# A dilated convolution: one of sixteen output images is stored in three transfers instead of one

## The chip, the cores and the metric

The kernel runs on one core of one Trainium2 chip. The metric is the device time of one execution in microseconds (us), as the median of several runs. Profiles are of one execution each.

## The reference

A 3x3 convolution with dilation 2 and zero padding of 2, in float32: 16 images of 64 channels and 64 x 64 pixels become 16 images of 128 channels of the same size.

```python
batch, c_in, h, w, c_out, k, dilation = 16, 64, 64, 64, 128, 3, 2
...
x_pad = np.pad(x, ((0, 0), (0, 0), (pad, pad), (pad, pad)), mode='constant')
...
output[b, co] += weight[co, ci, kh, kw] * x_pad[b, ci, kh*dilation:kh*dilation+h, kw*dilation:kw*dilation+w]
```

The inputs are 16.8 MB and the outputs 33.6 MB, so the kernel moves some 50 MB between memory and the core.

## The kernel before

The images are taken in eight pairs (`pb` = 0 to 7). A pair of input images of 64 channels fills the 128 partitions; TensorE works on both halves in turn (`hb` = 0, 1), 64 rows of the array for each.

Loads. The weights (line 63) and the pairs 0, 1 and 2 (line 71) are loaded from SyncE's queue, pair 0 in four pieces. Pair `pb + 3` is loaded from ScalarE's queue when pair `pb` begins. There are three float32 input buffers. GpSimd (line 126) and ScalarE (line 129) turn each pair into three float16 planes: even row groups, odd row groups, and their sum.

Weights. They are transposed by TensorE (line 106) into five slots: three rows of the 3x3 filter and two differences of rows. With the sum plane, an output row group takes five products instead of six: the one with the sum is shared by two row groups.

Main loop. Each pair has four units (`u`), each of 16 output rows for both images. In each unit TensorE (line 160) makes the shared product, which ScalarE copies out of the accumulator (line 181), then the two groups of difference products, to which VectorE adds the shared part (line 187) as it writes the result into the output buffer `o` of the image, 128 partitions (one for each output channel) of 64 x 64 float32. There are six such buffers, two for each pair.

Stores. After the last unit of a pair, SyncE issues the store of both images (line 198), 2 MB each: image `2 * pb + hb`, 128 rows of 16,384 bytes, one for each partition. The last pair is stored in two halves, after its second and its fourth unit, so the whole program has 18 stores. SyncE issues them in program order. Each waits for VectorE's last write into the buffer, and for the earlier transfer that had the same completion semaphore: the transfers of the program use eight of these in turn.

The order of the instructions is that of the program as written (a manual schedule).

Of the kernel before, what the change touches and what calls it, by code (L numbers as in the profile page):

```python
# [10 lines left out]
def kernel(  # L11
# [7 lines left out]
    nc = tc.nc  # L19

    B, CI, H, W = x.shape
# [5 lines left out]
    P = 128  # L27
    f32 = mybir.dt.float32
    f16 = mybir.dt.float16
    NP = B // 2  # L30
# [11 lines left out]
    NB = UQ * QW  # L42
    UR = 2 * UQ
    KWS = (1, 0, 2)

    SLOT = {"w0": 0, "w1": 1, "w2": 2, "w21": 3, "w01": 4}
    NS = len(SLOT)
# [20 lines left out]
    def load(pb, cuts, eng):  # L68
        x32[pb] = x32pool.tile([P, H, W], f32, tag="x32", name=f"x32_{pb}")
        for lo, hi in zip(cuts, cuts[1:]):  # L70
            eng.dma_start(out=x32[pb][:, lo:hi], in_=x_pair[pb, :, lo:hi])  # L71
# [21 lines left out]
    for name, a in (("w21", 2), ("w01", 0)):  # L93
        for u in range(2):
            nc.vector.tensor_sub(  # L95
                out=w16[:, SLOT[name] * KW : (SLOT[name] + 1) * KW, u, :],
# [5 lines left out]
    for n, name in enumerate(("w1", "w21", "w0", "w01", "w2")):  # L102
        ps = cpool.tile([P, NB], f32, tag="ps", name=f"wt{n}")
        k0 = SLOT[name] * KW
        for j in range(KW):
            nc.tensor.matmul(  # L106
                out=ps[:, j * CO : (j + 1) * CO],
# [12 lines left out]
    def prepare(pb, lo, hi):  # L120
        if pb not in x16:
            x16[pb] = x16pool.tile([P, 3, 2 * NQ, W], f16, tag="x16", name=f"x16_{pb}")
        q0, q1 = lo // 4, hi // 4
        src = x32[pb].rearrange("p (q e r) w -> p q e (r w)", e=2, r=2)
        dst = x16[pb].rearrange("p e (q r) w -> p q e (r w)", r=2)
        nc.gpsimd.tensor_add(  # L126
            out=dst[:, q0:q1, 2, :], in0=src[:, q0:q1, 0, :], in1=src[:, q0:q1, 1, :]
        )
        nc.scalar.copy(out=dst[:, q0:q1, 0:2, :], in_=src[:, q0:q1, :, :])  # L129
# [4 lines left out]
    def conv(pb, hb, ps, u, terms):  # L134
# [4 lines left out]
        for name, e, shift in terms:  # L139
            for kw in KWS:  # L140
                dw = (kw - 1) * d
# [14 lines left out]
    def phase(pb, u, terms):  # L156
        ps = [cpool.tile([CO, NB], f32, tag="ps", name=f"ps{hb}") for hb in range(2)]
        for pair in zip(*(conv(pb, hb, ps[hb], u, terms) for hb in range(2))):
            for m in pair:
                nc.tensor.matmul(**m)  # L160
        return ps

    for pb in range(NP):
        o = [
            opool.tile([P, H, W], f32, tag="o", name=f"o{pb}_{hb}") for hb in range(2)
        ]
        ov = [t.rearrange("p (q e r) w -> p q e (r w)", e=2, r=2) for t in o]
        last = pb == NP - 1
        for u in range(NU):
            if u == 0 and pb + 3 < NP:  # L170
                load(pb + 3, [0, H], nc.scalar)
            if pb + 1 < NP:
                if u == 1:
                    prepare(pb + 1, 0, 36)
                elif u == 2:
                    prepare(pb + 1, 36, H)

            s32 = []
            for hb, ps in enumerate(phase(pb, u, [("w1", 2, 0)])):
                s = spool.tile([P, NB], f32, tag="s32", name=f"s32_{hb}")  # L180
                nc.scalar.copy(out=s, in_=ps)  # L181
                s32.append(s)
            for e, terms in enumerate(
                ([("w21", 1, 0), ("w0", 1, -1)], [("w01", 0, 0), ("w2", 0, 1)])
            ):
                for hb, ps in enumerate(phase(pb, u, terms)):
                    nc.vector.tensor_add(  # L187
                        out=ov[hb][:, u * UQ : (u + 1) * UQ, e, :],
                        in0=ps.rearrange("p (q c) -> p q c", c=QW),
                        in1=s32[hb].rearrange("p (q c) -> p q c", c=QW),  # L190
                    )


            step = NU // 2 if last else NU
            if (u + 1) % step == 0:
                fl = slice((u + 1 - step) * 4 * UQ, (u + 1) * 4 * UQ)
                for hb in range(2):
                    nc.sync.dma_start(out=out[2 * pb + hb, :, fl], in_=o[hb][:, fl])


# [33 lines left out]
```

## Time and profile before

| | |
|---|---|
| time, median of 3 runs | 129.29 us (128.47 to 130.64) |
| the profiled execution's own time | 130.13 us |
| its span, first to last instruction | 128.3 us |
| moved by DMA | 50.77 MB, mean 396 GB/s |
| stores of 2,048 KB (14), issue to landing | 20.4 us, median |
| stores of 1,024 KB (4), issue to landing | 15.5 us, median |
| TensorE busy | 105.4 us (82%) |
| VectorE busy | 83.1 us (65%) |
| ScalarE busy | 67.4 us (52%) |
| GpSimd busy | 38.5 us (30%) |

The span is what the profile shows of an execution; the time has some 1.8 us more around it. An engine's busy time is a mean over the span. The page also cuts the span in 40 slices with a digit for each engine (tenths of the slice that it was busy), and gives the same for the core's 16 DMA engines, which carry out all transfers whatever engine issues them. A store's time to landing runs from its issue to the last of its sixteen completion marks, so it holds the time that it stands in the queue behind earlier transfers.

### The profile page before, as it was taken

The page shows a single profiled execution, that of the slowest core. Times are in us where ns is not written, and L with a number is a line of the kernel's source. Part 1 is how long each engine was busy: PE and PEld are TensorE (multiplying, and loading weights), DVE is VectorE, ACT ScalarE, POOL GpSimd, SP SyncE. Part 2 cuts the span into 40 slices and gives each one's busy share as a digit, 9 for nine tenths or more (in the row PEclk, how much of TensorE's full clock was granted, in tenths as well). Part 3 has the DMA queues.
Part 4 walks back from the last instruction along what each step waited for, and adds up shares of the span by engine and source line. Part 5 has one row for each costly group of instructions (what it writes and reads, how often), then busy time and mean ns, then how long its engine had stood idle before and what let it go on. Part 6 is the DMA issues. An engine that isn't in the chain of part 4 may idle for free.

```text
span 128.3 us, 2442 instructions
## 1 busy us (share of the span) xinstructions
PE 105.4 (82%) x981; PEld 55.3 (43%) x981; DVE 83.1 (65%) x136; ACT 67.4 (52%) x87; POOL 38.5 (30%) x24
## 2 busy tenths in 40 slices
PE   6399979999999999999999999999999999300000
PEld 2164425655565555555555555555556555100000
DVE  0550759887788778777877749978777777700000
ACT  3778597496359537933883398339833333000000
POOL 2095391499467006700860094000000000000000
PEclk9999999999999999999999999999999999995555
DMA  4999999998999999999999999999999999999940
GB/s 126 300 462 419 424 444 424 383 296 373 424 444 424 416 426 434 419 439 439 409 434 429 444 409 434 439 419 414 439 449 409 424 444 424 414 424 421 429 186 13
DMA packets 4330, 50.77 MB, mean 396 GB/s; under 512 B 480, under 2 KB 480, under 8 KB 1120
## 3 DMA queue, kind: packets, MB, share of 16 engines
q1 hardware_dynamic: 3600, 40.14, 74.6%
q10 hardware_dynamic: 720, 10.49, 20.4%
q8 instruction: 7, 0.11, 0.3%
q14 instruction: 3, 0.02, 0.0%
HBM read 17.07 MB, written 33.55 MB: 394 GB/s over the span
## 4 chain that ended last, share of the span: by engine, by line
PE 75%; ACT 7%; DMA 2%; DVE 1%; issue 1%; DVEq 0%; ACTq 0%
PE ps L160 74%; ACT x L129 3%; DMA w<-in_weight_dram 2%; ACT w L92 2%; ACT s L181 2%; PE wt L106 1%; DVE o L187 1%; DVEq L229 0%; ACT w_sb L117 0%; ACTq L71 0%; ACTq L181 0%; DVEq L187 0%
## 5 line engine op out<-in xcount | busy, mean ns | idle before, releaser
L160 PE MATMUL ps<-x,w_sb 64*128 64x496 f16 (+2 forms) x960 | 100.9, 368 | 1.6 <-ACT s L181 1.2
L187 DVE TENSOR_TENSOR o<-ps,s 128x512 f32<-128x512 f32 x128 | 79.5, 683 | 23.7 <-PE ps L160 14.8
L160 PEld LDWEIGHTS <-w_sb 64*128 64x128 f16 x960 | 53.0, 94 | 49.3 <-issue 3.9
L181 ACT COPY s<-ps 128x512 f32<-128x512 f32 x64 | 34.4, 589 | 36.6 <-issue 20.3
L126 POOL TENSOR_TENSOR x<-x 128x1152 f16<-128x1152 f32 (+4 forms) x18 | 37.8, 2124 | 39.2 <-PE ps L160 23.0
L129 ACT CAST x<-x 128x2304 f16<-128x2304 f32 (+4 forms) x18 | 30.7, 1720 | 1.5 <-DMA x<-in_x_dram 1.5
L86 PE MATMUL warm<-zero 128*128 128x512 f16 x6 | 2.7, 630 | 1.2 <-DVE zero L80 1.2
L106 PE MATMUL wt<-ident,w 128*128 128x128 f16 x15 | 1.8, 312 | 2.2 <-ACT w L92 2.2
L95 DVE TENSOR_TENSOR w<-w 128x192 f16<-128x192 f32 x4 | 1.7, 492 | 2.6 <-DMA w<-in_weight_dram 2.6
L92 ACT CAST w<-w 128x576 f16<-128x576 f32 x2 | 2.3, 1213 | 1.7 <-DMA w<-in_weight_dram 1.7
L106 PEld LDWEIGHTS <-w 128*128 128x128 f16 x15 | 1.5, 145 | 3.1 <-ACT w L92 3.1
L115 DVE CAST w_sb<-wt 128x384 f16<-128x384 f32 x3 | 1.7, 557 | 1.4 <-PE wt L106 1.2
L86 PEld LDWEIGHTS <-zero 128*128 128x128 f16 x6 | 0.7, 137 | 2.3 <-DVE zero L80 1.2
L92 ACT ACT_TABLE_LOAD x1 | 1.3, 1283 | 0.7 <-PEq L215 0.7
L117 ACT CAST w_sb<-wt 128x384 f16<-128x384 f32 x2 | 1.0, 478 | 1.1 <-PE wt L106 1.1
L80 DVE MEMSET zero<- 128x256 uint32 x1 | 0.3, 272 | 0.9 <-PEq L215 0.9
masks.py:199 POOL TENSOR_SCALAR_AFFINE_SELECT ident<-ident 128x128 f16<-128x128 f16 x1 | 0.3, 292 | 0.1
masks.py:197 POOL MEMSET ident<- 128x128 f16 x1 | 0.2, 204 | 0.3 <-POOLq L215 0.3
L215 POOL MEMSET const-float32-0.0<- 128x1 f32 x1 | 0.1, 99 | 0.2 <-issue 0.2
L215 POOL MEMSET const-bfloat16-1.0<- 128x1 bf16 x1 | 0.1, 102 | 0.0
L215 POOL MEMSET const-uint8-127<- 128x1 uint8 x1 | 0.1, 102 | 0.0
L215 POOL MEMSET const-float32-1.0<- 128x1 f32 x1 | 0.1, 99 | 0.0
## 6 DMA issues: line engine op xcount, KB each, us to landing
out_dram<-o SPq DMA_DIRECT2D x14, 2048.0 KB, 20.4
x<-in_x_dram ACTq DMA_DIRECT2D x5, 2048.0 KB, 14.8
x<-in_x_dram SPq DMA_DIRECT2D x2, 2048.0 KB, 16.2
out_dram<-o SPq DMA_DIRECT2D x4, 1024.0 KB, 15.5
x<-in_x_dram SPq DMA_DIRECT2D x2, 512.0 KB, 6.5
x<-in_x_dram SPq DMA_DIRECT2D x1, 640.0 KB, 5.2
x<-in_x_dram SPq DMA_DIRECT2D x1, 384.0 KB, 7.4
w<-in_weight_dram SPq DMA_DIRECT2D x1, 288.0 KB, 2.9
```

What stands on the lines that cost most here:

```text
L86: nc.tensor.matmul(out=warm, lhsT=zero[:, 0:P], rhs=zero, start=True, stop=True)
L92: nc.scalar.copy(out=w16[:, 0:NK, u, :], in_=w32k)
L95: nc.vector.tensor_sub(out=w16[:, SLOT[name] * KW : (SLOT[name] + 1) * KW, u, :], in0=w32k[:, a * KW : (a + 1) * KW, :], in1=w32k[:, KW : ...
L106: nc.tensor.matmul(out=ps[:, j * CO : (j + 1) * CO], lhsT=w16[:, k0 + j, :, :].rearrange("o t i -> o (t i)"), rhs=ident, start=True, stop= ...
L115: nc.vector.tensor_copy(out=dst, in_=ps[:, 0 : KW * CO])
L117: nc.scalar.copy(out=dst, in_=ps[:, 0 : KW * CO])
L126: nc.gpsimd.tensor_add(out=dst[:, q0:q1, 2, :], in0=src[:, q0:q1, 0, :], in1=src[:, q0:q1, 1, :])
L129: nc.scalar.copy(out=dst[:, q0:q1, 0:2, :], in_=src[:, q0:q1, :, :])
L160: nc.tensor.matmul(**m)
L181: nc.scalar.copy(out=s, in_=ps)
L187: nc.vector.tensor_add(out=ov[hb][:, u * UQ : (u + 1) * UQ, e, :], in0=ps.rearrange("p (q c) -> p q c", c=QW), in1=s32[hb].rearrange("p (q ...
L215: nc = _bacc.Bacc("TRN2", target_bir_lowering=False, num_devices=1)
```

## The change

Image 8 (`b == NP`, that is `pb` = 4, `hb` = 0) is stored in three transfers, which SyncE issues one after another: rows 14 to 63 of all 128 partitions, then rows 0 to 13 of the partitions 0 to 118, then rows 0 to 13 of the partitions 119 to 127. Every other image is stored as before. The bytes that are stored are the same.

```diff
+    R7 = 14
...
                 for hb in range(2):
-                    nc.sync.dma_start(out=out[2 * pb + hb, :, fl], in_=o[hb][:, fl])
+                    b = 2 * pb + hb
+                    if b == NP:
+                        parts = ((0, P, R7, H), (0, 119, 0, R7), (119, P, 0, R7))
+                    else:
+                        parts = ((0, P, fl.start, fl.stop),)
+                    for p0, p1, r0, r1 in parts:
+                        nc.sync.dma_start(
+                            out=out[b, p0:p1, r0:r1], in_=o[hb][p0:p1, r0:r1]
+                        )
```

## The prediction

> **What bounds the kernel now.** I read the slices of the span first, then the DMA queues, then the waits of SyncE, and last a few stretches at the end, because the slices show work going on long after the compute engines have stopped.
>
> The page's slices (40 of 3.2 us each) and its table of DMA queues:
>
> ```profile
> span 128.3 us, 2442 instructions
> PE   6399979999999999999999999999999999300000
> DVE  0550759887788778777877749978777777700000
> DMA  4999999998999999999999999999999999999940
> GB/s 126 300 462 419 424 444 424 383 296 373 424 444 424 416 426 434 419 439 439 409 434 429 444 409 434 439 419 414 439 449 409 424 444 424 414 424 421 429 186 13
> q1 hardware_dynamic: 3600, 40.14, 74.6%
> q10 hardware_dynamic: 720, 10.49, 20.4%
> q8 instruction: 7, 0.11, 0.3%
> ```
>
> TensorE and VectorE are done after slice 34 (the last VectorE instruction ends at 111.0 us), but the DMA engines are full from slice 1 to slice 37, at about 420 GB/s, and end in a ragged tail: 186 GB/s in slice 38, 13 in the last. So the sixteen DMA engines set the end. The packet counts tell how a transfer is dealt out. The kernel has 25 transfers on q1 and 5 on q10, each of 128 rows; 25 x 16 x 9 = 3600 and 5 x 16 x 9 = 720: each of the sixteen engines gets 8 data packets and one small completion mark of each, equal shares every time.
>
> What SyncE waits for:
>
> ```profile
> SPq L198 <- DVE o L187: 95.4, 18, 18.0
> SPq L229 <- DMA out_dram<-o: 14.7, 3, 9.9
> ```
>
> The stores wait for VectorE only, and the program's last instruction (L229) for the stores. And stretches at the end (start:end, length, the engines' busy times, granted clock, DMA share, GB/s):
>
> ```profile
> 118.00:120.00 2.00, 0.00 (x0) 0.00 (x0) 0.00 (x0) 0.00 (x0) 0.00 (x0) 0.50 1.02 430
> 121.70:124.62 2.92, 0.00 (x0) 0.00 (x0) 0.00 (x0) 0.00 (x0) 0.00 (x0) 0.50 0.57 238
> 124.65:126.90 2.25, 0.00 (x0) 0.00 (x0) 0.00 (x0) 0.00 (x0) 0.00 (x0) 0.50 0.06 25
> 126.95:128.30 1.35, 0.00 (x0) 0.00 (x0) 0.00 (x0) 0.00 (x0) 0.00 (x0) 0.50 0.00 0
> ```
>
> All sixteen engines work until about 121.8 us, fifteen of them stop between there and 124.6, and for the last 2.3 us the share is 0.06: one engine of sixteen (1/16 = 0.0625) still writes. Its last packet ends at 126.93. The trace's packet records show why. Of the 16 KB packets after 34 us nearly all take 611 ns, but one unbroken train, each packet starting as the one before it ends, takes 619 to 667 (mostly 644 to 653 from 73 us on); it returns to 611 when the compute engines stop, near 110. One engine is thus some 6% slower while the kernel computes, and every byte on it is on the path to the end. The completion marks say the same: image 8's store has its sixteen marks between 88.0 and 92.2 us, the last 1.3 behind the fifteenth; in the last store that gap is 2.4.
>
> **The change part by part.** Image 8's store (pb 4, hb 0) becomes three transfers: rows 14 to 63 by 128 partitions (12,800 bytes a row), rows 0 to 13 by 119 partitions and by 9 (3,584 bytes a row). Bytes and arithmetic stay the same, and each compute engine's list of instructions is the same.
>
> Packet prices. The trace has 121 ns for 3,072 bytes, 159 for 4,096, 309 for 8,192, 611 for 16,384; neighbours in a full train overlap by about 3. In between lies 137 for 3,584 and 476 for 12,800; a full row is 608 in the train.
>
> How 119 rows are dealt out no row shows, since all transfers of before have 128. Bounds: evenly over sixteen (8 each, one with 7), each engine gets 8 x 476 + 8 x 137 plus at most one of the nine rows, less 8 x 608 = 4.86 us: +0.18 us everywhere. All on one engine: 119 x 137 = 16.3 us, less 4.86 - 3.81 = 1.06 saved, so +15.2. I take what keeps the equal shares that the rows show: 119 = 7 x 17, so seven engines with 17 rows each, and nine engines with one row each. Then, against 4.86 us before:
> - a crowded engine (seven): 3.81 + 17 x 0.137 + 0.14 + two marks of 9 ns = 6.29, so +1.43 us;
> - an engine with one of the nine rows only (two): 3.81 + 0.14 = 3.95, so -0.91;
> - the others (seven): 3.81, so -1.06.
>
> The Trainium skill (DMA: Bandwidth & Descriptors, "Why a DMA increments its semaphore by 16 and not by 1") states that the largest number of engines up to 16 that divides the slowest dimension is used, on this path the lowest-numbered ones. By that the shares are the 7 and 9 above, and the seven are engines 0 to 6; no run here has shown such a transfer yet.
>
> What this does to the end. From image 8's store on, the queues hold nothing but stores (the last load lands at 73.4 us, image 8's store is issued at 73.9), and each engine has work waiting until it ends: a microsecond taken from an engine moves its own end by that. If the slow engine is one of the nine that lose work, it ends at 126.93 - 1.0 = 125.9. The latest of the others ended at 124.61; if crowded, it ends at 126.04. So the end comes at about 126.0, and 0.9 us are gained.
>
> What I cost at nothing, with its cover:
> - Two more issues on SyncE. The second store of a pair takes up to 0.95 us to issue, so image 9's store goes out some 1.9 us later, at about 76.4. Engines reach it after image 8's, at 88 or later: 11 us of cover. Without that cover it would be 1.9 us.
> - Waits on reused completion semaphores. The eight are taken in turn, so two more transfers shift every later store's predecessor. The built program's lists give them: the tightest is image 9's store, which now waits for image 4's store (landed 69.8, issue at 74.5); the 119-row part waits for image 3's store and the 9-row part for the load of pair 6 (61.5 and 61.2); the last store waits for image 9's (97.4 against 111.6). Behind a late one, only further stores would stand on SyncE.
> - The output buffers: six, so VectorE writes pair 7 into those of images 8 and 9, first at 99.7 and about 100.3. They landed at 92.2 and 97.4. Crowded engines would land image 9 at 95.7 + 1.4 = 97.2. VectorE is not held.
>
> Sum against the profiled execution: 130.13 - 0.9 = 129.2 us (its span 128.3, and 1.8 around it). It lies 0.84 above the median of the runs shown, 129.29, so I forecast 128.4 for the median.
>
> **The rivals.**
> - The slow engine is one of the seven crowded ones. Then it gets 1.43 x 1.06 = 1.5 us more and ends at 128.4: 131.6 for the profiled execution, 130.8 as a median, slower than before. For it: no record carries an engine's number, and seven of sixteen are crowded. Against it: nine of sixteen are not. The same time comes out, by a few tenths less, if the slow train belongs to profiled executions alone, since then a crowded engine is the last.
>
>   The Trainium skill (same page, "Latency and other measured facts") says that engines 7 and 15 are usually slower than the rest in traces. That would put the slow engine outside the seven, and the sum would be the forecast's; the trace has one such engine, not two, and does not number it.
> - The 119 rows are spread over sixteen. Then nothing moves but 0.18 us: 129.5. For it: no equal share fits sixteen, and a ragged deal would be the simplest. Against it: all thirty transfers here have equal shares.
> - The 119 rows go to one engine. It decides as soon as one engine has over 2.3 us more than the others, and it would have 15: 144.5. For it: nothing but the missing common divisor with 16. Against it: 119 has a divisor, 7.
>
> **How the numbers follow.** Seven and nine shares: 0.82, by the equal shares. Slow engine outside the seven: 9 of 16, so 0.47 for the forecast with the rounding, 0.35 for the slower case of 130.8; 0.13 for the even spread, 0.03 for the single engine, 0.02 for what I haven't thought of. The predicted time is that of the likeliest, 128.4, its own range 127.5 to 129.5 (the runs shown lie 0.8 below and 1.4 above their median). The range reaches to 130.8, to take in the even spread and half of the slower case. 2% is 2.6 us, about what a measurement of this kernel can tell from no change; none of the likely cases reaches it alone. Faster by over 2%: 0.04, runs of the forecast that scatter low. Slower by over 2%: 0.06, the single engine and a few of the slower case. Within: 0.90.
>
> **What would show it.** In the packet records: 128 packets of 3,584 bytes near 137 ns and 128 of 12,800 near 479. In the completion marks: if seven engines are crowded, the spread between the first and last engine of a store grows by about 2.5 us behind image 8 for engines that are crowded against those that are not, and stays so to the last store; with an even deal it stays as it is, with one engine it is 15. At the end: if the forecast is right, the stretch in which one engine alone works shrinks from 2.3 us to a few tenths, with the last packet near 126.0. If one engine still works alone for 3 us or more, the slow one is among the crowded. Any wait of SyncE for an output DMA ahead of L229's counterpart, or of VectorE for a store, would prove my covers wrong.

## The result and the profile after

The changed kernel takes 130.28 us (median of 22 runs, 129.12 to 131.80) where the kernel before takes 128.83 (22 runs, 127.78 to 130.67). The ratio is 1.0092, with an interval of 1.0067 to 1.0118: slower by about 1.2 us. The ratio leaves out executions that lie over 1.5% above the fastest of their kernel, which is why it is nearer to 1 than the two medians, 1.45 us apart. The forecast was faster by 0.9; the first rival said slower by 1.5.

The single profiles say the opposite at first sight. That of the changed kernel (an execution of 129.19 us) has a span 0.9 us shorter than that of before. From its page, the span, the slices and the queues:

```profile
span 127.4 us, 2445 instructions
DMA  4999999999999999999999999999999999999940
GB/s 141 305 449 417 432 432 442 417 401 412 427 437 432 419 424 427 422 427 432 422 432 427 437 422 422 427 419 408 423 427 432 417 422 424 430 412 422 414 190 15
q1 hardware_dynamic: 3744, 40.14, 75.6%
q10 hardware_dynamic: 720, 10.49, 19.5%
```

The difference comes from a place that the change does not touch. In slices 7 to 9 (22 to 32 us) the profile of before moved 383, 296 and 373 GB/s, this one 417, 401 and 412. The same stretch in numbers, first before, then changed:

```profile
23.00:32.00 9.00, 9.00 (x92) 4.91 (x89) 7.25 (x13) 6.75 (x8) 7.73 (x4) 1.00 0.98 346
```

```profile
23.00:32.00 9.00, 9.00 (x90) 4.80 (x88) 7.26 (x13) 6.75 (x8) 7.42 (x4) 1.00 1.00 413
```

67 GB/s over 9 us are 0.6 MB, or 1.4 us at 430 GB/s. Executions differ by that, and a second profile of the changed kernel (below) has 346 there and a span of 129.2:

```profile
23.00:32.00 9.00, 9.00 (x92) 4.91 (x90) 7.94 (x14) 6.55 (x9) 5.99 (x3) 1.00 0.97 346
```

So the two kernels have to be compared from image 7's store on, the last one ahead of the change. On the slow DMA engine its data ends at 86.5 us before and at 84.2 after, 2.3 us ahead; the last completion mark of the program comes at 127.38 and at 126.57, only 0.8 ahead. Between the two, 1.5 us were lost, and all of it in image 8's store: the slow engine needs 5.17 us from its first row to image 9's first row before and 6.66 after, and from there to the last mark 35.27 and 35.28.

How the rows were dealt out stands in the packet count of q1. 24 uncut transfers and the 128-partition part have 25 x 16 x 9 = 3600 packets; 119 rows with seven marks and 9 rows with nine marks make 144 more: 3744. The completion marks agree: seven for the 119-row part, 88.7 to 91.2 us, nine for the other. The short rows take 140 ns, the 12,800-byte rows 479.

Stretches at the end of the changed kernel's profile (start:end, length, the engines' busy times, granted clock, DMA share, GB/s):

```profile
121.70:124.62 2.92, 0.00 (x0) 0.00 (x0) 0.00 (x0) 0.00 (x0) 0.00 (x0) 0.50 0.33 137
124.65:126.00 1.35, 0.00 (x0) 0.00 (x0) 0.00 (x0) 0.00 (x0) 0.00 (x0) 0.50 0.06 24
```

Again a share of 0.06, one engine, to the last packet at 126.11. And its train of slow packets can be followed through image 8's store: eight rows of 12,800 bytes from 84.18, then short rows until 90.84, where image 9's 16 KB rows begin. From 88.24 to 90.84 are 2.60 us: 17 short rows, a mark, one more short row and its mark, each row some 0.143. From there the train goes on unbroken to the last packet. The slow engine is a crowded one.

SyncE's waits in the changed kernel:

```profile
SPq L207 <- DVE o L188: 95.6, 18, 18.0
SPq L240 <- DMA out_dram<-o: 14.2, 5, 4.6
SPq L207 <- DMA x<-in_x_dram: 1.9, 1, 1.9
```

The stores still wait for VectorE, and L240 (L229 before) for the stores. The one wait for a load, 1.9 us, ends at 6.0 us, long before the first store; the kernel before has the same one (2.4 us).

### The profile page after: what moved, and what is told of

Read it like the earlier page. It is cut to its first block, busy times and chain, and to the rows that moved or that the text cites. A ratio compares the mean times of both kernels' runs of the same rounds, so it can differ in the third digit from the quotient of the medians.

```text
span 127.4 us, 2445 instructions
## 1 busy us (share of the span) xinstructions
PE 106.3 (83%) x981; PEld 55.9 (44%) x981; DVE 83.3 (65%) x136; ACT 67.4 (53%) x87; POOL 38.5 (30%) x24
## 4 chain that ended last, share of the span: by engine, by line
PE 80%; ACT 2%; DMA 2%; DVE 1%; issue 1%; DVEq 0%
PE ps L161 79%; DMA w<-in_weight_dram 2%; ACT w L93 2%; PE wt L107 1%; DVE o L188 1%; DVEq L240 0%; ACT s L182 0%; DVEq L188 0%
## 5 line engine op out<-in xcount | busy, mean ns | idle before, releaser
L161 PEld LDWEIGHTS <-w_sb 64*128 64x128 f16 x960 | 53.7, 95 | 48.2 <-issue 3.2
```

## The experiments

The theory: one DMA engine is slower than the other fifteen and sets the end; the 119-row part gives it 1.43 us more, 1.5 with its slower packets. The rivals: the cut itself costs the time (two more transfers, short rows, longer issues); or the slow engine is another one in every execution, and what ends last is whatever is crowded. All ratios are to the kernel before, run beside it on the same chip.

**Same three transfers, nobody crowded.**

```diff
-parts = ((0, P, R7, H), (0, 119, 0, R7), (119, P, 0, R7))
+parts = ((0, P, R7, H), (0, 112, 0, R7), (112, P, 0, R7))
```

> The same three transfers with the same row sizes, but the top 14 rows are cut at partition 112: 112 = 16 x 7 and 16 = 16 x 1, so every DMA engine gets 8 short rows. First theory (one slow DMA engine is among the seven that the 119-row transfer crowds, and the end follows its bytes): each engine gets 8 x 476 + 8 x 137 less 4,864 ns = +0.06 us, ratio to before 1.000 to 1.002, and the train of slow packets ends as far behind the rest as before. Rival (the split itself costs it: two more transfers, 128 more packets, longer issues on SyncE): the cost stays, ratio near 1.009.

Measured: 0.9991 (0.9953 to 1.0029). Two more transfers and 128 more packets cost nothing that can be seen; it is the deal. The lone engine's stretch at the end is there:

```profile
125.15:126.45 1.30, 0.00 (x0) 0.00 (x0) 0.00 (x0) 0.00 (x0) 0.00 (x0) 0.50 0.06 25
```

**Fifteen engines and one relieved.**

```diff
+parts = ((0, P, R7, H), (0, 120, 0, R7), (120, P, 0, R7))
```

> The cut is at partition 120: 120 = 15 x 8 and 8 = 8 x 1. Fifteen engines keep about their work (+0.06 us, eight of them +0.20), one loses 1.06 us. First theory (the slow engine is one of the seven lowest): ratio 1.000 to 1.003, since it is not relieved. Rival (the slow engine is the one that is relieved, the last of sixteen): its end comes 1.06 us earlier, ratio near 0.993, and the alone stretch at the end shrinks to about 1 us.

Measured: 1.0027 (0.9996 to 1.0059). The end does not come a microsecond earlier, so the engine that this cut relieves is not the slow one. In its profile one engine ends alone by only 0.58 us, which by itself would look like the rival; but the slow train spends 5.36 us on image 8, so it has its share of the short rows.

**Twice the rows.**

```diff
-    R7 = 14
+    R7 = 28
```

> The cut of the changed kernel with twice the rows (28 instead of 14) in the parts of 119 and 9 partitions: 9,216 and 7,168 bytes a row, 344 and 268 ns. A crowded engine gets 8 x 344 + 18 x 268 + 18 - 4,864 = +2.73 us, the slow one 6% more, 2.9. First theory (a slow crowded engine is last anyway, so each added byte counts): ratio to before about 1.022, twice the changed kernel's loss. Rival (the split itself costs it, by the number of transfers): 1.009 as for 14 rows.

Measured: 1.0276 (1.0195 to 1.0357), 3.5 us where 2.9 were expected; the interval holds both. Only four executions were timed, and the median of all four, 133.70, lies 4.8 above the 128.93 of before. With the number of transfers unchanged the loss grows with the rows, but by more than the packet prices say. In the profile the slow train needs 14.41 us from image 8's first row to image 10's first row, against 10.32 before: 4.1 more, not 2.9. Between 88 and 94.5 us 21 of the rows of 7,168 bytes take 336 to 925 ns, where 272 is usual. Why is open.

**Numbering the slow engine.**

```diff
+cut = {8: 6, 9: 5, 10: 4, 11: 3, 12: 2, 13: 1}.get(b)
+if cut:
+    parts = ((0, P, 2, H), (0, cut, 0, 2), (cut, P, 0, 2))
```

> One look, to number the slow engine. Images 8 to 13 store their top two rows (512 bytes) in two transfers, cut at partition 6, 5, 4, 3, 2 and 1. With equal shares over the lowest-numbered engines, the number of short rows on an engine in these six images is: engine 0: 62, 42, 32, 26, 10, 128; 1: 62, 42, 32, 26, 10, 0; 2: 1, 42, 32, 26, 9, 0; 3: 1, 1, 32, 25, 9, 0; 4: 1, 1, 0, 25, 9, 0; 5: 1, 0, 0, 0, 9, 0; 6 to 13: 0, 0, 0, 0, 9, 0; 14 and 15: none. First theory (the slow engine is one of the seven): the train of slow packets shows one of the first six patterns or that of engine 6. Rival (it is one of the nine others, or the slow engine changes from run to run): the pattern of 7 to 15, with none or only the nine.

Measured (one execution, 133.13 us): the slow train (rows of 15,872 bytes at 615 to 646 ns, where the packet prices give 592) has gaps behind its eight rows of image 8 and of image 9 that fit one short row of 24 ns each, none behind image 10 (the next row starts 2 ns after), and 0.6 us behind image 11, which is 25 short rows. 1, 1, 0, 25 is, of the patterns expected, that of engine 4 alone.

**Taking work off engine 4.**

```diff
-    R7 = 14
+    R7 = 5
...
+parts = ((0, P, R7, H), (0, 124, 0, R7), (124, P, 0, R7))
```

> A cut that takes work off the slow engine, if it is engine 4 as the run with six cuts numbers it: the top 5 rows of image 8 are cut at partition 124 = 4 x 31, the rest 4 = 4 x 1, so both short transfers lie on engines 0 to 3. Those get 8 x 561 + 32 x 51 + 18 - 4,864 = +1.27 us, all others 8 x 561 - 4,864 = -0.38, the slow one -0.40. First theory (the slow engine is always number 4 and sets the end): the end comes about 0.4 us earlier, ratio near 0.997, and the gap between the last and the fifteenth completion mark of the last store shrinks by some 0.4 us, or by more where one of the four crowded is the fifteenth. Rival (any cut over few engines is slower, since the crowded ones end last): ratio 1.005 to 1.010.

Measured: 0.9970 (0.9935 to 1.0004). In its profile the slow train goes from image 8's last long row straight to image 9's first row, at 89.89 us, with no short row between. The end:

```profile
121.70:123.75 2.05, 0.00 (x0) 0.00 (x0) 0.00 (x0) 0.00 (x0) 0.00 (x0) 0.50 0.52 220
123.80:125.20 1.40, 0.00 (x0) 0.00 (x0) 0.00 (x0) 0.00 (x0) 0.00 (x0) 0.50 0.11 47
125.30:125.58 0.28, 0.00 (x0) 0.00 (x0) 0.00 (x0) 0.00 (x0) 0.00 (x0) 0.50 0.07 29
```

A share of 0.11 is two engines. The slow train ends at 125.23 us and another engine, by the sum a crowded one, at 125.62: the slow engine is no longer the last. With 8 rows:

> The same with 8 rows: engines 0 to 3 get 8 x 533 + 32 x 80 + 18 - 4,864 = +1.98 us, the others 8 x 533 - 4,864 = -0.60, the slow one -0.64. First theory: ratio 0.995 as long as none of the four crowded engines comes to lie behind the slow one (it was 1.4 to 2.4 us behind the next in the profiles so far, so 2.0 + 0.6 is about where they meet): 0.995 to 1.003. Rival (crowded engines end last): 1.010 to 1.015.

Measured: 0.9997 (0.9959 to 1.0035), inside the first theory's span. Here the slow train leaves image 9 with the mark at 94.86, and the last mark of that store, 96.71, is a crowded engine's: what engine 4 gained, one of engines 0 to 3 took. At the end the slow train stops at 124.54, and another engine works alone until 126.30:

```profile
124.60:126.25 1.65, 0.00 (x0) 0.00 (x0) 0.00 (x0) 0.00 (x0) 0.00 (x0) 0.50 0.06 25
```

The 5 rows a second time:

> The cut at 124 with 5 rows a second time, since its interval reached 1.000. First theory (0.4 us taken off engine 4, which sets the end): 0.997 again, and with both runs together an interval below 1. Rival (nothing is gained, the first was scatter): 1.000 to 1.003.

Measured: 0.9957 (0.9908 to 1.0007). Each interval reaches 1. Weighted by their widths, both together give about 0.9966, with an interval of 0.994 to 0.999 if the two are independent; but the medians of all executions, 128.42 against 128.73 and 128.65 against 128.78, have ratios of 0.998 and 0.999. So a gain is likely but not shown. The profile of this second run also has another engine at the end: the slow train stops at 124.58, and one engine works alone until 125.60:

```profile
124.65:125.55 0.90, 0.00 (x0) 0.00 (x0) 0.00 (x0) 0.00 (x0) 0.00 (x0) 0.50 0.06 27
```

What is shown is that crowding four other engines for 1.3 us each costs nothing like the 1.005 to 1.010 of the rival: the slow engine was 1.3 to 2.3 us behind the next one in the profiles of before and of the cut at 112. And 3 rows:

> The same with 3 rows: 8 x (61 rows, 15,616 bytes, 580 ns) - 4,864 = -0.22 us for engine 4 and -0.24 with its slower packets, engines 0 to 3 +0.95 us. First theory: ratio 0.998. Rival (crowded engines end last): 1.003 to 1.007.

Measured: 0.9999 (0.9957 to 1.0041). A gain of 0.002 can't be told apart from none here; a loss of 0.003 to 0.007 is not supported by the middle, and its lower end lies within the interval. Here the slow engine is the last again, 1.10 us behind the next.

**Both kernels once more.**

> The changed kernel once more, for a second profile. First theory: ratio 1.009, its slow train carries 17 + 1 short rows behind image 8's eight long ones (2.5 us), and its last completion mark stands alone. Rival (the slow engine is another one in each execution): the train carries one short row or none in this profile.

Measured: 1.0116 (1.0072 to 1.0160). The slow train has its eight long rows from 85.98 and image 9's first row at 92.62: 6.65 us, against 6.66 in the first profile. Its lone stretch:

```profile
126.60:127.85 1.25, 0.00 (x0) 0.00 (x0) 0.00 (x0) 0.00 (x0) 0.00 (x0) 0.50 0.06 26
```

> The kernel before once more, one look, for a second profile: the slow train (16 KB packets of 644 to 653 ns while the compute engines work) is there again and ends 1.4 to 2.5 us behind the other engines. If the train is missing, the first profile was a special case.

Measured (one execution, 129.84 us): the train is there (16 KB rows of 634 to 667 ns up to 110 us), and the last mark comes 1.84 us after the fifteenth. Lone stretch:

```profile
124.85:126.60 1.75, 0.00 (x0) 0.00 (x0) 0.00 (x0) 0.00 (x0) 0.00 (x0) 0.50 0.06 23
```

**Why that engine is slow.**

```diff
+        total = 1
-        for name, e, shift in terms:
-            for kw in KWS:
+        for name, e, shift in terms[:1]:
+            for kw in KWS[:1]:
```

> The kernel before with only the first matmul of each accumulation (192 of 960 in the main loop, so most of the products are left out); transfers, copies and additions as before. One look at why one DMA engine is slow. If TensorE's stream of instructions takes time from it (it ran at full speed once the compute engines had ended), its packets of 16 KB are near 611 to 625 ns instead of 644 to 653, and it lies less than 1 us behind the others in the last store. If it is slow whatever the engines do, the packets stay near 650.

Measured (one execution, 127.24 us): one train again, but of 616 to 648 ns, mostly 625, and 0.28 us behind the others in the last store. The page's first lines:

```profile
span 125.4 us, 901 instructions
PE 79.1 (63%) x213; PEld 15.8 (13%) x213; DVE 80.9 (65%) x136; ACT 68.2 (54%) x87; POOL 38.3 (31%) x24
```

With 768 matmuls and 768 weight loads fewer, some 2% of slowness are left of 6 (625 against 611). So most of it goes when most of TensorE's instructions go. That the instructions are the cause is not shown: this run also ended its compute earlier and had a granted clock of 1.0, and whether it would be the stream of instructions or the recording of them was not tried.

**The slow train at image 8.** From the first row of image 8's store to the first of image 9's, on the slow engine:

| cut | us | against before | worked out |
|---|---|---|---|
| none (before), two profiles | 5.17 | | |
| 119, 14 rows (changed), two profiles | 6.66, 6.65 | +1.48 | +1.5 |
| 112, 14 rows | 5.24 | +0.07 | +0.06 |
| 120, 14 rows | 5.36 | +0.19 | +0.20 |
| 124, 3 rows | 4.95 | -0.22 | -0.24 |
| 124, 5 rows, two profiles | 4.78 | -0.39 | -0.40 |
| 124, 8 rows | 4.55 | -0.62 | -0.64 |

Sums of packet prices come out within 0.03 us for these cuts; for the 28 rows of the third run they don't (4.1 against 2.9, above). Under the rival that the slow engine changes from execution to execution, these profiles would not all show a share that engine 4 has in the cut; they do.

## Why the prediction was wrong, point by point

- **What bounds the kernel: right.** Sixteen DMA engines, one of them some 6% slower. It was there in every profile with all the matmuls, with the same packets, and it was the last in all whose end was followed but those of the cuts at 124 with 5 and with 8 rows.
- **How 119 rows are dealt out: right.** Seven engines with 17 rows and nine with one, by the packet count of q1. The Trainium skill (DMA: Bandwidth & Descriptors, "Why a DMA increments its semaphore by 16 and not by 1") has the rule for this, the largest number up to 16 that divides the rows, and says that the engines are the lowest-numbered; the seven marks and the numbering run agree with it. (In the bound for an even deal, 119 rows over sixteen engines are 8 on seven of them and 7 on nine, not "8 each, one with 7"; the +0.18 us stays the most that an engine gets.)
- **Packet prices: right.** 476 and 137 ns in a train were taken; the records show 479 and 140, which overlap by 3.
- **What was costed at nothing: right.** Image 9's store was issued at 76.2 us, 76.4 had been worked out. Neither SyncE nor VectorE waited for a store ahead of the end, and the cut at 112 with the same issues and waits costs nothing (0.9991).
- **Which side the slow engine is on: wrong.** This is the step that failed. "If the slow engine is one of the nine that lose work" was taken on a count of nine out of sixteen, 0.47 against 0.35, with no row that numbers an engine. It is engine 4, one of the seven. The number itself hangs on the rule of the lowest-numbered engines; what the runs show without it is that the slow engine has a share in the parts cut for 5, 6, 7 and 15 engines, and none in those cut for 4. The first rival is what happened, 1.5 us on the slow engine, measured as 1.48 in the trace and as 0.9 to 1.5 in the runs (1.0067 to 1.0118 of 128.83).
- The Trainium skill's sentence on engines 7 and 15 (same page, "Latency and other measured facts") would have put it outside the seven. In this kernel the trace has one slow engine, and it is number 4. The page itself calls its guess at the cause specific to SWDGE, transfers issued from GpSimd; those here are issued from SyncE and ScalarE.
- **The sign for a crowded slow engine: wrong.** "3 us or more" alone at the end doesn't follow from the prediction's own sums: 128.4 for the slow engine and 126.04 for the latest of the other crowded ones are 2.4 apart, since those end later too. The two profiles of the changed kernel have 1.8 and 1.2 us. What told was the number of short rows in the slow train.
- **Whether the engine is slow only where the profiler records: open.** The timed executions that the record lists one by one all have a span and a granted clock, so none of them shows an execution that isn't recorded.
- **The median: off for a second reason.** The prediction scaled the profile's time to the median of three runs, 129.29; 22 runs have 128.83. And the early stretch, 346 or 413 GB/s, moves an execution by as much as the change does, so one profile of each kernel gave the wrong sign.

## What to carry to other kernels

When DMA engines set the end, look past their mean: a share of 0.06 in the last stretch is one engine alone, and then only that engine's bytes count, until another engine is as late: the 8 rows cut at 124 took 0.6 us off the slow one and gained nothing (0.9997). A transfer over a number of partitions that sixteen doesn't divide loads some engines more; before such a cut is used to even out the work, a run with a few short rows cut at different partitions numbers the slow engine at the cost of one profile. And two profiles are compared from the last point ahead of the change, not by their spans.

## What the runs showed of the hardware that was not expected

Packets can get a little slower in general after such a cut, and not only on the slow engine. Between 112 and 121 us, where the slow train is back to the usual time, the mean packet takes 1.000 of its usual time (611 ns for 16 KB, 309 for 8 KB) before (two profiles) and with the cut at 112, 1.007 in both profiles of the changed kernel, and 1.010 with 28 rows. Engines that are out of step don't explain it by themselves: the cuts at 124 load four engines more as well, and have 1.000 with 3 rows, 1.003 and 1.005 with 5, and less than 1.001 with 8; the cut at 120 has 1.001. Over these 9 us 1.007 to 1.010 are 0.06 to 0.09 us on each engine, far too little for the 28-row run's excess, which the slow train shows earlier, while its short rows are written. No run took either apart.
